# Layer 1's attention scores: split queries and keys over 128 rows instead of plain products over 64

## The chip, the cores and the metric

The kernel runs on one core of a Trainium2 chip as one program. The metric is device time in microseconds (us); the median of several executions is compared. One execution of each kernel was also recorded by the hardware profiler, and all rows below come from such a recording. Engines are named as in the profile: PE is TensorE (PEld its weight loads), DVE is VectorE, ACT is ScalarE, POOL is GpSimd, and SP issues most loads.

## The reference, cut to what matters

The network has a first block and, behind it, a second block of two layers over 256 latent tokens and 256 context tokens. The change lies in the differential attention of the second block's last layer. There are 8 heads; each has two components of 64 dimensions for queries and keys. In the last layer only the 256 latent tokens are queries, and all 512 tokens are keys.

```python
def diff_attend(q, k, v, lam):
    s = jnp.einsum('bqhcd,bkhcd->bchqk', q, k).astype(jnp.float32) * (ATT_HEAD_DIM ** -0.5)
    p = jax.nn.softmax(s, axis=-1)
    a = p[:, 0] - lam * p[:, 1]
    return jnp.einsum('bhqk,bkhe->bqhe', a.astype(v.dtype), v)
...
    att_l, att_c = diff_attention(apply_rope(qk(ql), cos, sin), apply_rope(qk(kl), cos, sin), vv(vl),
                                  qk(qc), qk(kc), vv(vc), lam, lam_init, subln_g, with_ctx_out)
```

## The kernel before

**Number forms.** The kernel keeps the accuracy of float32 in its large products by splitting both operands into a high part, rounded to the type float32r, and a low part, the rest. `mm3` (L156 to L158) then adds three products: high by high, high by low, low by high. Weights come through `slab`: a load on SP's queue into `wr`, a cast on ScalarE into `wh` (L150), a subtraction on VectorE into `wl` (L151), three buffers each. `fm` makes one such product over all 1024 input features, into a PSUM bank with the tag `lin`, of which there are two in this stage.

**The attention of a layer** is `attention`, called with `last=False` in layer 0 and `last=True` in layer 1. Layer 0 has 512 queries (four tiles of 128 in each head), layer 1 has 256 (two tiles). For each head, `proj` makes the queries (even index) and the keys (odd index) of both components, 64 rows each, in one tile of 128 rows: `fm`, a copy out of PSUM (L1030), four copies of 32 rows that swap halves (L1033), and three operations on VectorE for the rotation (L1034 to L1036). `parts` then splits this tile in layer 0. Keys: in component 0's tile, rows 0 to 63 hold the high part and rows 64 to 127 the low part, and for component 1 the other way round. Queries: one tile holds the high part twice, a second one (`lows`) holds the low part in one half and zeros in the other. Two products over 128 rows then give high by high, high by low, and low by high. In layer 1, `parts` returns the tile as it is, and `scores` multiplies it as plain float32, component 0 on rows 0 to 63, component 1 on rows 64 to 127 (L1071).

**A tile's chain.** `scores` writes two PSUM banks (tag `sc`, two buffers, so the next tile's scores wait for this tile's exponentials). `weights` takes each maximum (L1084), the exponential with its sum on ScalarE (L1086), and the combined weights on VectorE (L1088 to L1093). `values` transposes them on TensorE (L1099), copies them (L1101) and multiplies them by V (L1105). The loop over tiles (L1150) starts a tile's successor before it finishes the tile, and puts in other work for TensorE: the next projection, or `cover`, which runs steps of `ssd_out` (the output projection of the other branch, L156 to L158 with `yh` and `w_ssd_o`). `finish` normalizes a head; its transposes (L1120) are put into a later tile, for the last head behind the gate products `ga`.

**Order.** The order of instructions on each engine is set by a scheduling layer when the program is built, from all instructions and their dependences; each engine then works in that order. So an edit can move instructions far from it.

Of the kernel before, what the change touches and what calls it, by code (L numbers as in the profile page):

```python
# [9 lines left out]
F32 = mybir.dt.float32  # L10
F32R = mybir.dt.float32r
# [1006 lines left out]
def attention(C, l, H, V, neglam, gsub, ao, last, cover):  # L1018


    nc, A = C.nc, C.A
    mm = nc.tensor.matmul
    W = A["wqk"][l]
    NQ = 256 if last else 512
    nt = NQ // 128

    def proj(i, N):
        ps = C.fm([W[i]], lambda k: (H(k)[0][:, :N], H(k)[1][:, :N]), N)
        t = C.t("qk" if last else "qt", [128, N])
        nc.scalar.copy(t, ps)  # L1030
        sw = C.t("sw", [128, 256])
        for b in range(4):
            nc.scalar.copy(sw[32 * b:32 * b + 32, :], ps[32 * (b ^ 1):32 * (b ^ 1) + 32, 0:256])  # L1033
        nc.vector.tensor_tensor(t[:, 0:256], t[:, 0:256], C.cos, ALU.mult)  # L1034
        nc.vector.tensor_tensor(sw, sw, C.sin, ALU.mult)
        nc.vector.tensor_tensor(t[:, 0:256], t[:, 0:256], sw, ALU.add)  # L1036
        return t

    def parts(i, N):


        t = proj(i, N)
        if last:
            return t
        a, b = slice(0, 64), slice(64, 128)
        hi = [C.t("qk", [128, N], F32R) for _ in range(2)]
        if i % 2:
            nc.scalar.copy(hi[0][a], t[a])
            nc.vector.tensor_tensor(hi[0][b], t[a], hi[0][a], ALU.subtract)
            nc.scalar.copy(hi[1][b], t[b])  # L1050
            nc.vector.tensor_tensor(hi[1][a], t[b], hi[1][b], ALU.subtract)
            return hi
        lo = lows[i // 2 % 2]
        nc.scalar.copy(hi[0][a], t[a])
        nc.scalar.copy(hi[1][b], t[b])
        nc.scalar.copy(hi[0][b], t[a])
        nc.scalar.copy(hi[1][a], t[b])
        nc.vector.tensor_tensor(lo[0][a], t[a], hi[0][a], ALU.subtract)
        nc.vector.tensor_tensor(lo[1][b], t[b], hi[1][b], ALU.subtract)
        return hi, lo  # L1060

    def scores(q, k, tq):
        k0, nk = (0, 4) if tq < 2 else (2, 2)
        n = nk * 128
        r = []
        tok, keys = slice(tq * 128, (tq + 1) * 128), slice(k0 * 128, 512)
        for c in range(2):
            sc = C.p("sc")[:, :n]
            row = slice(c * 64, c * 64 + 64)
            if last:  # L1070
                mm(sc, q[row, tok], k[row, keys], start=True, stop=True)  # L1071
            else:
                mm(sc, q[0][c][:, tok], k[c][:, keys], start=True, stop=False)
                mm(sc, q[1][c][:, tok], k[c][:, keys], start=False, stop=True)
            r.append(sc)
        return r, k0, nk

    def weights(sc, n):
        pr = C.t("pr", [128, 2, 512])
        m = C.t("sm", [128, 2])  # L1080
        m8 = C.t("sm", [128, 2])
        den = C.t("sm", [128, 2])
        for c in range(2):
            nc.vector.tensor_reduce(m[:, c:c + 1], sc[c], AX.X, ALU.max)  # L1084
            nc.vector.tensor_scalar(m8[:, c:c + 1], m[:, c:c + 1], -0.125, None, ALU.mult)
            nc.scalar.activation(pr[:, c, :n], sc[c], AF.Exp, bias=m8[:, c:c + 1], scale=0.125, accum_out=den[:, c:c + 1])  # L1086
        r = C.t("sm", [128, 2])
        nc.vector.reciprocal(r, den)  # L1088
        rl = C.t("sm", [128, 1])
        nc.vector.tensor_tensor(rl, r[:, 1:2], neglam, ALU.mult)  # L1090
        a = C.t("at", [128, 512])
        nc.vector.tensor_scalar(a[:, :n], pr[:, 0, :n], r[:, 0:1], None, ALU.mult)
        nc.vector.scalar_tensor_tensor(a[:, :n], pr[:, 1, :n], rl, a[:, :n], ALU.mult, ALU.add)  # L1093
        return a

    def values(a, k0, nk, h, tq, ob, ss, v):
        tp = C.p("tr")
        for i in range(nk):
            nc.tensor.transpose(tp[:, i * 128:(i + 1) * 128], a[:, i * 128:(i + 1) * 128], C.ident)  # L1099
        aT = C.t("aT", [128, 512])  # L1100
        nc.scalar.copy(aT[:, :nk * 128], tp[:, :nk * 128])  # L1101
        cover()
        po = C.p("o")
        for i in range(nk):
            mm(po[:, 0:128], aT[:, i * 128:(i + 1) * 128], v[:, k0 + i, h % 2 * 128:(h % 2 + 1) * 128], start=i == 0, stop=i == nk - 1)  # L1105
        nc.scalar.copy(ob[:, tq, :], po[:, 0:128])
        jk = C.t("at", [128, 128])
        nc.scalar.activation(jk, ob[:, tq, :], AF.Square, accum_out=ss[:, tq:tq + 1])

    def finish(h, ob, ss):  # L1110
        v = C.t("sm", [128, 4])
        nc.vector.tensor_scalar(v[:, :nt], ss[:, :nt], 1.0 / 128, 1e-6, ALU.mult, ALU.add)
        r = C.rsqrt(v[:, :nt], nt)
        for tq in range(nt):
            nc.vector.tensor_scalar(ob[:, tq, :], ob[:, tq, :], r[:, tq:tq + 1], None, ALU.mult)

        def put(tag="tr"):
            tp = C.p(tag)
            for tq in range(nt):
                nc.tensor.transpose(tp[:, tq * 128:(tq + 1) * 128], ob[:, tq, :], C.ident)  # L1120
            nc.scalar.activation(ao(h), tp[:, :NQ], AF.Copy, scale=gsub)
        return put

    lows = []
    if not last:
        lows.extend([C.keep([128, NQ], F32R, name="ql") for _ in range(2)] for _ in range(2))
        for pair in lows:
            nc.gpsimd.memset(pair[0][64:128].bitcast(F32), 0.0)
            nc.gpsimd.memset(pair[1][0:64].bitcast(F32), 0.0)
    todo = [(h, tq) for h in range(8) for tq in range(nt)]  # L1130

    chunks = [(2 * h + i, (NQ, 512)[i]) for h in range(8) for i in range(2)]
    ready = {}

    def project():
        if chunks:
            i, N = chunks.pop(0)
            ready[i] = parts(i, N)

    def start(i):  # L1140
        h, tq = todo[i]
        return scores(ready[2 * h], ready[2 * h + 1], tq)

    project()
    project()
    put, vs = None, [V(0), V(1)]
    sc, k0, nk = start(0)
    if last:
        project()
    for i, (h, tq) in enumerate(todo):  # L1150
        if tq == 0:
            if h in (2, 4):
                vs.append(V(h // 2 + 1))
            ob = C.t("ob", [128, 4, 128])
            ss = C.t("sm", [128, 4])
        a = weights(sc, nk * 128)
        if tq < 2 and chunks:
            project()
        else:
            cover()  # L1160
        if tq == 0 and put:
            put()
        kk = k0, nk
        if i + 1 < len(todo):
            sc, k0, nk = start(i + 1)
        values(a, *kk, h, tq, ob, ss, vs[h // 2])
        if tq == nt - 1:
            put = finish(h, ob, ss)
    cover()
    return put  # L1170
# [36 lines left out]
def layer(C, l, pre, get_x, vec, mods, neglam, init, H, last, enter=None, sums=None):  # L1207
# [27 lines left out]
    with C.phase(f"l{l}", gT=(NQ, max(ng, 1))):  # L1235
# [90 lines left out]
        with C.phase(f"a{l}", ao=(NQ, 8), ob=(512, 2)):  # L1326
            aos = [C.t("ao", [128, NQ]) for _ in range(8)]
            C.psum(**PS["ah"])
            with C.phase(f"ah{l}", skip=24 if last else 40, V=(1024, 2), qk=(512, 8), qt=(512, 1), sw=(256, 2), pr=(1024, 2), at=(512, 3), aT=(512, 2),
                         yr=(NQ, 2), yh=(NQ, 12 if last else 11)):  # L1330
                so = ssd_out(C, l, yd, vec, T1, NQ)
                def V(j):
                    v = C.t("V", [128, 4, 256])
                    nc.gpsimd.dma_start(v, vd[:, :, j * 256:(j + 1) * 256])
                    return v

                ry = C.rstd_steps(acc, NQ, 2048, rsy)
                steps = iter(COVER[last])

                def cover():  # L1340
                    next(ry, None)
                    for _ in range(int(next(steps, 0))):
                        next(so, None)

                put = attention(C, l, H, V, neglam, gsub, lambda k: aos[k], last, cover)
                for _ in so:
                    pass
# [462 lines left out]
```

## Time and profile before

| | |
|---|---|
| three runs | 2458.41, 2455.89, 2449.28 us |
| median | 2455.89 us |
| profiled execution | 2455.91 us, of which the recorded span is 2454.1 us |
| PE busy | 2394.6 us of the span (98%), mean granted clock 0.995 |
| DVE, ACT, POOL busy | 1737.9 (71%), 1379.5 (56%), 185.6 (8%) |
| layer 1's scores (L1071) | 64 records, 2028.1 to 2174.3 us of the span |

Busy time is the union of an engine's recorded instructions. Matmuls overlap in their pipeline, so the distance between the starts of two matmuls tells what one costs, and its own duration does not. Layer 1's attention lies at about 2017 to 2190 us of the span, layer 0's at about 840 to 1072.

### The profile page before, as it was taken

Reading aid. Unit: us, or ns where it says so; the run is one execution under the profiler, and the core shown is the slowest. Engines: PE = TensorE matmul, PEld = TensorE weight load, DVE = VectorE, ACT = ScalarE, POOL = GpSimd, SP = SyncE. Lnnn points to the kernel's source line nnn. Section 1 sums busy time; section 2 is a strip of 40 time slices with the busy share of each in tenths; the row PEclk is TensorE's granted clock in tenths of the full one; section 3 lists DMA queues with packets and bytes.
Section 4 is the critical chain, followed back from the end, with each engine's and each line's share of the span. In section 5 each row is a group of like instructions: output and inputs, shape, how many; then the busy total and the mean of one; then the engine's idle time right before and its main releaser. Section 6 shows DMA issues by size and latency. Waiting matters only on the chain. (4 is left out here: it accounts for less than half of the span.)

```text
span 2454.1 us, 40285 instructions
## 1 busy us (share of the span) xinstructions
PE 2394.6 (98%) x15330; PEld 2023.8 (82%) x15330; DVE 1737.9 (71%) x3336; ACT 1379.5 (56%) x2793; POOL 185.6 (8%) x426
## 2 busy tenths in 40 slices
PE   7999999999999999999999999999999999999998
PEld 7869998877777777788888777899788887789997
DVE  6558757698888778873485334467888887887776
ACT  5445545577687677743353223245776766655553
POOL 2000000122122100000100000001211210000000
PEclk9999999999999999999999999999999999999999
DMA  7537775645545422233467553346555553346654
GB/s 272 173 129 235 254 261 167 211 133 155 155 134 170 139 82 82 78 90 95 122 234 259 169 172 135 96 154 199 181 153 161 181 163 105 103 139 206 182 187 130
DMA packets 117585, 395.53 MB, mean 161 GB/s; under 512 B 15360, under 2 KB 21232, under 8 KB 117392
## 3 DMA queue, kind: packets, MB, share of 16 engines
q1 hardware_dynamic: 96768, 328.35, 41.6%
q0 software_dynamic: 20624, 64.62, 9.5%
q8 instruction: 120, 1.97, 0.3%
q14 instruction: 73, 0.60, 0.1%
HBM read 378.34 MB, written 14.05 MB: 160 GB/s over the span
## 5 line engine op out<-in xcount | busy, mean ns | idle before, releaser
L150 ACT CAST wh<-wr 128x1024 fp32r<-128x1024 f32 (+2 forms) x509 | 530.5, 1042 | 654.5 <-PE lin L157 544.4
L151 DVE TENSOR_TENSOR wl<-wr,wh 128x1024 fp32r<-128x1024 f32 (+2 forms) x509 | 617.5, 1215 | 340.0 <-ACT wh L150 332.6
L156 PE MATMUL lin<-hh,wh 128*128 128x512 f32 (+2 forms) x1296 | 476.4, 368 | 2.3 <-ACT sw L1033 1.7
L157 PE MATMUL lin<-hl,wh 128*128 128x512 f32 (+2 forms) x1296 | 467.5, 361 | 0.3 <-DVE hl L1556 0.3
L158 PE MATMUL lin<-hh,wl 128*128 128x512 f32 (+2 forms) x1296 | 466.4, 360 | 0.1
L156 PEld LDWEIGHTS lin<-hh,wh 128*128 128x128 f32 (+1 forms) x1296 | 243.3, 188 | 48.7 <-issue 5.7
L158 PEld LDWEIGHTS lin<-hh,wl 128*128 128x128 f32 (+1 forms) x1296 | 243.0, 188 | 39.0 <-issue 1.2
L157 PEld LDWEIGHTS lin<-hl,wh 128*128 128x128 f32 (+1 forms) x1296 | 243.3, 188 | 38.3 <-issue 2.5
L889 DVE SCALAR_TENSOR_TENSOR cy<-xp,cw,cy 128x512 f32<-128x512 f32 (+1 forms) x256 | 181.4, 714 | 11.4 <-ACT cy L887 6.4
L156 PE MATMUL lin<-nh,wh 128*128 128x258 f32 (+2 forms) x576 | 185.2, 322 | 0.5 <-ACT wh L150 0.5
L158 PE MATMUL lin<-f,wl 128*128 128x256 f32 (+1 forms) x576 | 182.7, 318 | 1.8 <-DVE wl L151 1.8
L157 PE MATMUL lin<-nl,wh 128*128 128x258 f32 (+2 forms) x576 | 184.0, 319 | 0.1
L158 PE MATMUL lin<-nh,wl 128*128 128x258 f32 (+2 forms) x576 | 184.0, 320 | 0.0
L156 PE MATMUL lin<-f,wh 128*128 128x256 f32 (+1 forms) x576 | 183.7, 319 | 0.2 <-ACT f L161 0.2
L157 PE MATMUL lin<-f,wh 128*128 128x256 f32 (+1 forms) x576 | 182.8, 318 | 0.0
L156 PE MATMUL lin<-xh,wh 128*128 128x256 f32 (+1 forms) x472 | 135.2, 287 | 11.0 <-ACT wh L150 10.3
L158 PE MATMUL lin<-xh,wl 128*128 128x256 f32 (+1 forms) x472 | 132.4, 281 | 1.3 <-DVE wl L151 1.3
L157 PE MATMUL lin<-xl,wh 128*128 128x256 f32 (+1 forms) x472 | 132.3, 280 | 0.0
L156 PEld LDWEIGHTS lin<-nh,wh 128*128 128x128 f32 x576 | 109.3, 190 | 20.3 <-issue 5.0
L156 PEld LDWEIGHTS lin<-f,wh 128*128 128x128 f32 x576 | 109.2, 190 | 15.3 <-issue 3.4
L158 PEld LDWEIGHTS lin<-f,wl 128*128 128x128 f32 x576 | 109.6, 190 | 9.4 <-DVE wl L151 2.0
L158 PEld LDWEIGHTS lin<-nh,wl 128*128 128x128 f32 x576 | 109.3, 190 | 7.6 <-DVE wl L151 0.2
(444 smaller groups left out, 5274.8 us busy)
## 6 DMA issues: line engine op xcount, KB each, us to landing
wr<-in_w_mlp SPq DMA_DIRECT2D x144, 512.0 KB, 4.4
aw<-in_ada_w SPq DMA_DIRECT2D x96, 512.0 KB, 5.0
wr<-in_wxbc SPq DMA_DIRECT2D x64, 512.0 KB, 4.4
BC<-dcs POOLq DMA_DIRECT2D x96, 256.0 KB, 5.2
wr<-in_w_out SPq DMA_DIRECT2D x32, 512.0 KB, 3.7
wr<-in_wv SPq DMA_DIRECT2D x32, 512.0 KB, 4.2
EC<-der POOLq DMA_DIRECT2D x64, 256.0 KB, 5.0
wr<-in_wz SPq DMA_DIRECT2D x32, 512.0 KB, 6.3
```

Source lines behind the costliest of these rows:

```text
L150: nc.scalar.copy(hi[:, :n], raw[:, :n])
L151: nc.vector.tensor_tensor(lo[:, :n], raw[:, :n], hi[:, :n], ALU.subtract)
L156: mm(out, sh, mh, start=first, stop=False)
L157: mm(out, sh, ml, start=False, stop=False)
L158: mm(out, sl, mh, start=False, stop=last)
L889: nc.vector.scalar_tensor_tensor(cy, xp[:, :, k:k + 256], w(k), cy, ALU.mult, ALU.add)
```

## The change

Layer 1 takes the same path as layer 0. Every projection goes through the tile `qt` (one buffer) and is split into high and low parts; the eight buffers `qk` then hold two tiles for each projection instead of one. Four tiles `lows` for the queries' low parts are made, with their unused halves set to zero on GpSimd. Each component's scores are two products over 128 rows, 512 columns each, in float32r.

```diff
@@ -1026,7 +1026,7 @@
 
     def proj(i, N):
         ps = C.fm([W[i]], lambda k: (H(k)[0][:, :N], H(k)[1][:, :N]), N)
-        t = C.t("qk" if last else "qt", [128, N])
+        t = C.t("qt", [128, N])
         nc.scalar.copy(t, ps)
         sw = C.t("sw", [128, 256])
         for b in range(4):
@@ -1040,8 +1040,6 @@
 
 
         t = proj(i, N)
-        if last:
-            return t
         a, b = slice(0, 64), slice(64, 128)
         hi = [C.t("qk", [128, N], F32R) for _ in range(2)]
         if i % 2:
@@ -1066,12 +1064,8 @@
         tok, keys = slice(tq * 128, (tq + 1) * 128), slice(k0 * 128, 512)
         for c in range(2):
             sc = C.p("sc")[:, :n]
-            row = slice(c * 64, c * 64 + 64)
-            if last:
-                mm(sc, q[row, tok], k[row, keys], start=True, stop=True)
-            else:
-                mm(sc, q[0][c][:, tok], k[c][:, keys], start=True, stop=False)
-                mm(sc, q[1][c][:, tok], k[c][:, keys], start=False, stop=True)
+            mm(sc, q[0][c][:, tok], k[c][:, keys], start=True, stop=False)
+            mm(sc, q[1][c][:, tok], k[c][:, keys], start=False, stop=True)
             r.append(sc)
         return r, k0, nk
 
@@ -1121,12 +1115,10 @@
             nc.scalar.activation(ao(h), tp[:, :NQ], AF.Copy, scale=gsub)
         return put
 
-    lows = []
-    if not last:
-        lows.extend([C.keep([128, NQ], F32R, name="ql") for _ in range(2)] for _ in range(2))
-        for pair in lows:
-            nc.gpsimd.memset(pair[0][64:128].bitcast(F32), 0.0)
-            nc.gpsimd.memset(pair[1][0:64].bitcast(F32), 0.0)
+    lows = [[C.keep([128, NQ], F32R, name="ql") for _ in range(2)] for _ in range(2)]
+    for pair in lows:
+        nc.gpsimd.memset(pair[0][64:128].bitcast(F32), 0.0)
+        nc.gpsimd.memset(pair[1][0:64].bitcast(F32), 0.0)
     todo = [(h, tq) for h in range(8) for tq in range(nt)]
 
     chunks = [(2 * h + i, (NQ, 512)[i]) for h in range(8) for i in range(2)]
```

In layer 1 each even projection so has four casts of 64 x 256 on ScalarE and two subtractions of 64 x 256 on VectorE behind the rotation, each odd one two casts and two subtractions of 64 x 512. Lines behind the edit have smaller numbers after the change: L1093 and L1099 are the transposes and the value products there, L1052 to L1055 and L1046, L1048 the casts.

The scheduling layer gives TensorE, VectorE and ScalarE another order from this stage's start to its end; SP's order stays, and GpSimd's gains the four memsets alone. Two places follow. On ScalarE, where the first head's queries (`qk_21294`, after: `qt_21302`) and keys are prepared, before:

```order
L1030 COPY qk_21294<-lin_21263 128x256
L1033 COPY sw_21296<-lin_21263 32x256 x4
L1183 ACTIVATE yh_21494<-yr_21492,vec_2324 128x256
L1183 ACTIVATE yh_21500<-yr_21498,vec_2324 128x256
L150 CAST wh_21517<-wr_21516 128x1024
L1030 COPY qk_21335<-lin_21304 128x512
L1033 COPY sw_21337<-lin_21304 32x256 x4
```

The same place after the change, down to the casts of the keys:

```order
L1030 COPY qt_21302<-lin_21271 128x256
L1033 COPY sw_21304<-lin_21271 32x256 x4
L1175 ACTIVATE yh_21534<-yr_21532,vec_2324 128x256
L1175 ACTIVATE yh_21540<-yr_21538,vec_2324 128x256
L1052 CAST qk_21312<-qt_21302 64x256
L1053 CAST qk_21313<-qt_21302 64x256
L1054 CAST qk_21312<-qt_21302 64x256
L1055 CAST qk_21313<-qt_21302 64x256
L150 CAST wh_21557<-wr_21556 128x1024
L1030 COPY qt_21351<-lin_21320 128x512
L1033 COPY sw_21353<-lin_21320 32x256 x4
```

The four casts of the queries now stand ahead of the copies that empty the keys' PSUM bank. The second place is the end of the stage on TensorE: the last tile's transposes (`tr_23280`) and value products (`o_23341`), with products of `ssd_out` between them. Before:

```order
L156 MATMUL lin_23402<-yh_22997,wh_23397 128x256
L1099 MATMUL tr_23280<-c_ident,at_23250 128x128 x4
L157 MATMUL lin_23402<-yh_22998,wh_23397 128x256
L158 MATMUL lin_23402<-yh_22997,wl_23398 128x256
L156 MATMUL lin_23402<-yh_23048,wh_23397 128x256
L157 MATMUL lin_23402<-yh_23049,wh_23397 128x256
L158 MATMUL lin_23402<-yh_23048,wl_23398 128x256
L156 MATMUL lin_23402<-yh_23141,wh_23397 128x256
L157 MATMUL lin_23402<-yh_23142,wh_23397 128x256
L158 MATMUL lin_23402<-yh_23141,wl_23398 128x256
L1105 MATMUL o_23341<-V_22395,aT_23285 128x128 x4
```

After the change, from the last tile's scores (`sc_23327` and `sc_23330`) over the tile before it (`tr_23333`, `o_23380`) to its own transposes and value products (`tr_23432`, `o_23493`):

```order
L1067 MATMUL sc_23327<-qk_23075,qk_22927 128x512
L1068 MATMUL sc_23327<-qk_23075,ql_21265 128x512
L157 MATMUL lin_23568<-yh_23349,wh_23549 128x256
L158 MATMUL lin_23568<-yh_23348,wl_23550 128x256
L1067 MATMUL sc_23330<-qk_23076,qk_22928 128x512
L1068 MATMUL sc_23330<-qk_23076,ql_21266 128x512
L1093 MATMUL tr_23333<-c_ident,at_23273 128x128 x4
L1099 MATMUL o_23380<-V_22499,aT_23338 128x128 x4
L1093 MATMUL tr_23432<-c_ident,at_23402 128x128 x4
L1099 MATMUL o_23493<-V_22499,aT_23437 128x128 x4
```

All products of `ssd_out` now stand ahead of the last scores' second half; behind it the two tiles' transposes and value products follow each other, and then the gate products `ga`.

## Rows read from the trace of the kernel before

**Rows 1.** The page's first part, TensorE's share of it.

```profile
PE 2394.6 (98%) x15330; PEld 2023.8 (82%) x15330; DVE 1737.9 (71%) x3336; ACT 1379.5 (56%) x2793; POOL 185.6 (8%) x426
```

**Rows 2.** Windows: length, busy PE, PEld, DVE, ACT, POOL, PEclk, DMA, GB/s.

```profile
2017.00:2190.00 173.00, 164.11 (x1025) 132.64 (x1024) 135.66 (x373) 115.54 (x272) 3.04 (x5) 0.99 0.39 121
840.00:1072.00 232.00, 222.55 (x1117) 174.05 (x1116) 187.24 (x520) 171.81 (x420) 1.50 (x2) 1.00 0.27 83
2020.00:2030.00 10.00, 7.07 (x39) 4.91 (x38) 5.67 (x10) 7.19 (x15) 0.00 (x0) 0.93 0.71 242
```

**Rows 3.** Timeline of TensorE, layer 1: start, duration, line, tiles, shape, [idle before].

```profile
2062.99 0.28 PE L157 MATMUL lin<-hl,wh 128*128 128x256 f32 x1
2063.11 0.28 PE L158 MATMUL lin<-hh,wl 128*128 128x256 f32 x1
2063.31 1.13 PE L1071 MATMUL sc<-qk,qk 64*128 64x512 f32 x4
2064.37 0.39 PE L156 MATMUL lin<-yh,wh 128*128 128x256 f32 x1
2064.59 0.28 PE L157 MATMUL lin<-yh,wh 128*128 128x256 f32 x1
...
2173.73 1.12 PE L1071 MATMUL sc<-qk,qk 64*128 64x512 f32 x2
2174.78 0.39 PE L157 MATMUL lin<-yh,wh 128*128 128x256 f32 x1
```

**Rows 4.** Line L1071: its window (PE, PEld busy), and TensorE's idle time before it.

```profile
2017.00:2190.00 173.00, 23.07 (x64) 7.21 (x64) 0.99 0.39 121
...
  ACT pr L1086: 3.5, 8
```

**Rows 5.** Timeline of TensorE, layer 0's first scores.

```profile
844.36 0.50 PE L1073 MATMUL sc<-qk,qk 128*128 128x512 f32 x1 [0.61 <-DVE qk L1049]
844.70 0.40 PE L1074 MATMUL sc<-qk,ql 128*128 128x512 f32 x1
844.93 0.40 PE L158 MATMUL lin<-yh,wl 128*128 128x512 f32 x1
```

**Rows 6.** Tile qt, layer 0: ns min/median/max, first and last start.

```profile
L1048 ACT CAST qk<-qt x8: 602/617/623, 842.6 to 1028.7; 64x512 fp32r<-64x512 f32 x8
L1049 DVE TENSOR_TENSOR qk<-qt,qk x8: 684/685/686, 843.6 to 1029.8; 64x512 fp32r<-64x512 f32 x8
```

**Rows 7.** Lines by form, 2190 to 2200 us: busy us, mean ns | idle before.

```profile
L161 ACT CAST ah<-ao 128x256 fp32r<-128x256 f32 x8 | 2.9, 404 | 0.0
L162 DVE TENSOR_TENSOR al<-ao,ah 128x256 fp32r<-128x256 f32 x8 | 3.4, 426 | 0.0
```

**Rows 8.** Waits, 2017 to 2190 us: us in total, times, longest.

```profile
ACT pr L1086 <- DVE sm L1085: 28.9, 12, 3.9
DVE sm L1088 <- ACT pr L1086: 13.2, 13, 2.0
```

**Rows 9.** Timeline of TensorE at the stage's start.

```profile
2025.52 0.50 PE L156 MATMUL lin<-hh,wh 128*128 128x512 f32 x1 [1.51 <-ACT sw L1033]
...
2030.67 0.63 PE L156 MATMUL lin<-hh,wh 128*128 128x512 f32 x1
2031.10 0.63 PE L157 MATMUL lin<-hl,wh 128*128 128x512 f32 x1
```

**Rows 10.** Timeline of VectorE and TensorE, the last tile's chain.

```profile
2179.78 1.28 DVE L1084 TENSOR_REDUCE sm<-sc 128x1 f32<-128x512 f32 x2
...
2184.81 0.60 PE L1099 MATMUL tr<-c_ident,at 128*128 128x128 f32 x4
2185.16 0.37 PE L157 MATMUL lin<-yh,wh 128*128 128x256 f32 x1
...
2186.36 1.16 PE L1105 MATMUL o<-V,aT 128*128 128x128 f32 x8
2187.28 0.36 PE L156 MATMUL lin<-yh,wh 128*128 128x256 f32 x1
```

## The prediction

> **What bounds the kernel now.** The page's first part comes first: TensorE is busy for 98% of the span [rows 1], so a change pays only where it shortens TensorE's own work or a wait of TensorE. The windows view then cuts out the stage that the change touches, layer 1's attention, from 2017 to 2190 us of the span [rows 2]. Of these 173 us TensorE is busy for 164.1, VectorE for 135.7, ScalarE for 115.5. So TensorE is idle for 8.9 us here, and 2.9 of them lie in the first ten, where the first heads' queries and keys are prepared (7.07 of 10 busy). The other 6.0 are spread over sixteen tiles. Layer 0's attention already works in the split form, and the same view shows it from 840 to 1072 us: TensorE 222.6 of 232, idle 4.1%, with VectorE at 81% and ScalarE at 74%. It is the nearest thing to a trace of the changed kernel.
>
> **What the scores cost TensorE now.** A tile (128 queries of a head) has two plain products, one on rows 0 to 63 and one on rows 64 to 127, each recorded as two matmuls. Four records together hold TensorE for 1.06 us, from 2063.31 to the next start at 2064.37, and the one product that stands alone at 2173.73 holds it for 1.05 [rows 3]. So the two halves run at the same time, and a pair costs what one costs. Around a pair the stream stumbles: starts are 0.12 us apart in the stream, but 0.20 going in and 0.22 coming out, some 0.19 too much. All of the scores keep TensorE busy for 23.1 us [rows 4]. That is more than 16 x 1.06 = 17, because in several tiles the second half waits for the exponentials to free its bank: 3.5 us of waits in 8 places [rows 4], more inside the pairs. There are 17 groups (the last tile's halves stand apart). Each record ends about 0.07 after the next may start, so the scores take 23.1 - 17 x 0.07 + 17 x 0.19 = 25.1 us of TensorE's time.
>
> **What they cost after.** Layer 0 shows the new form: after the first product, which takes 0.34 behind a wait, the starts are 0.23 apart for 512 columns [rows 5]. A tile has four (two components, high and low queries): 64 x 0.23 = 14.7 us, and 16 x 0.11 for the first of each tile makes 16.5. The saving is at most 25.1 - 16.5 = 8.6 us. At least it is what the pairs cost without waits: 16 x (1.06 + 0.19) = 20.0, less 16.5, that is 3.5, if every wait inside a pair comes back as a wait between the new products. I take the middle, 6.
>
> The Trainium skill speaks against the change here: "TensorEngine Tiling (Array Packing)", Theoretical Speedup, gives up to 2x where the contracted dimension is 64 or less, and products over 128 rows give that up. The trace agrees that the two halves overlap (1.06 for both, 1.05 for one). The same page, Key Properties, says that a switch of the tiling mode drains TensorE, which agrees with the 0.20 and 0.22 beside 0.12. By the first rule together with "FP8 and Floating Point Precision", TensorE Precision Notes (true FP32 is four passes), streaming alone would be 4 x 512 columns before and after, a saving of nothing but the switches.
>
> **What is added on ScalarE and VectorE.** For each head the queries need four casts on 64 x 256 and two subtractions, the keys two casts on 64 x 512 and two subtractions. Layer 0 has the key's sizes: 0.617 us a cast, 0.686 a subtraction [rows 6]. No row has 64 x 256; between 128 x 256 (0.404 and 0.426 [rows 7]) and 64 x 512 (0.617 and 0.686) I take the lower, since the columns agree, and keep the upper for the range. ScalarE: 8 x (4 x 0.404 + 2 x 0.617) = 22.8 us. VectorE: 8 x (2 x 0.426 + 2 x 0.686) = 17.8 us (21.9 at the upper end). The stage would then have VectorE at (135.7 + 17.8)/173 = 89% and ScalarE at 80%: above layer 0's 81% and 74%, and below full. Both have gaps to put this in: 13.2 us in which VectorE waits for the exponentials and 28.9 in which ScalarE waits for the maxima [rows 8]. The cover is there on the average but not at every tile, since both engines work in order. If TensorE's idle share in the tiles goes from 6.0/163 = 3.7% towards twice layer 0's 4.1%, it costs between 0.7 and 7.4 us. I take 2, near layer 0's share, as its work is the same in kind.
>
> The queue of SP issues the same loads in the same order. GpSimd's four memsets stand ahead of the loads of V on its queue; the first value products come only after a whole tile's softmax, so they cost nothing. The copy into qt has one buffer now; layer 0 works with the same one, and its list of waits names no copy waiting for a subtraction. Nothing.
>
> **The start of the stage.** On ScalarE the four casts of the first queries are put ahead of the copies that free the bank of the first keys (the order listing of ScalarE). In the trace TensorE waits 1.51 us for just these copies, until 2025.52 [rows 9]. Four casts of 0.404 move that to 2027.1: 1.6 us more. After the wait the matmuls start 0.43 apart instead of 0.23 [rows 9], in a stretch with a mean granted clock of 0.93 [rows 2]: the lower level, 1.2 GHz, after idle time. That exists already. The first scores then wait for casts and subtractions of the keys, but ten products of the next projection now stand ahead of them, where it was four. I take 1.6, with 0.5 and 4 as the ends.
>
> **The end of the stage.** This is the piece that the diff alone doesn't show. Before, 51 projection products stand between the last two tiles (from the value products of the one to the transposes of the other), and more before and behind. After, they are used up earlier: behind the last scores come only two transposes and two value products, with nothing between (the order listing of TensorE). From the last tile's maxima at 2179.78 to the end of its value products, 0.92 us after 2186.36, the chain takes 7.5 us in the trace [rows 10]. TensorE has left to do there: 0.46 of scores, two transposes of 0.35 and two value products of 0.92, 3.0 us. So 4.5 us are idle. The finish of the last head then has 48 products (5.5 us) as cover where it had 63 (7.2 us): 0.5 more. Sum 5, between 3 (without the filler that VectorE ran inside that chain) and 8 (if the clock falls as at the start).
>
> **Sum.** -6 + 2 + 1.6 + 5 = +2.6 us. The profiled execution took 2455.91 us (span 2454.1, 1.8 around it) and the median of the three runs is 2455.89, so no correction: **2458 us**. The three runs lie 9 us apart, and about 0.5% (12.3 us) is what a measurement of this kernel can tell from no change.
>
> **The rivals.**
> *A, the work is hidden and TensorE keeps its gain.* No more idle time in the tiles, 8.6 saved, 1.6 at the start, 3 at the end: -4, 2452 us. For it: the gaps of [rows 8]. Against it: the last tile's bare chain. Chance 0.25.
> *B, VectorE becomes the bound.* Its idle time was 173 - 135.7 = 37.3 us. In my forecast the stage lasts 175.6 us and VectorE needs 153.5, so its idle time must shrink to 22.1. If none of it can be filled, because each wait for an exponential stays in the order, the stage grows by 17.8: 2474 us, slower by 0.7%. It decides for slower by 0.5% from 32 us of idle time on. For it: VectorE at 89% in order. Against it: layer 0 runs at 81% and loses 4.1% on TensorE. Chance 0.17, of which 0.1 is beyond 0.5%.
> *C, the products gain nothing but the switches.* If the four products of a tile take the pair's 1.06 us, because of waits between them, TensorE saves 16 x (0.19 - 0.11) = 1.3 us: 2455.9 - 1.3 + 8.6 = 2463 us. The streaming rule of the Trainium skill above would give this. For it: the waits for banks. Against it: the 0.23 of [rows 5]. Chance 0.15.
> My forecast has 0.43, with a range of its own from 2454 to 2463.
>
> **How the numbers follow.** The range reaches 3 us below A and 2 above half of B (2455.9 + 8.9 = 2465), for the spread of the runs: 2449 to 2467. Slower by over 0.5% (above 2468.2) is B's worse part, 0.10. Faster by over 0.5% (below 2443.6) needs all of the 8.6 and much of the idle 8.9 as well: 0.04. The rest, 0.86, is within.
>
> **What would show it.** In the trace after: the scores' products 0.23 apart, about 16 us in sum; VectorE near 153 us in the stage; TensorE's wait for the copies at the start about 3 us; a hole of 4 to 5 us in TensorE between the last scores and the gate products. I am wrong if VectorE's queue holds up the weights' low parts (waits of the third product of a group), if the hole is not there, or if a wait for a tile of the stage before shows up at the first copies, since the new tiles move the others in memory.

## The result, and the profile after

Six executions of the changed kernel had a median of 2478.63 us (2477.02 to 2481.99), and six of the kernel before 2453.2. The ratio is 1.0106, with a 95% interval from 1.009 to 1.0121: slower by 1.1%, about 25 us. The forecast was 2458, within 2449 to 2467.

The first part of the page of the changed kernel answers to [rows 1]:

```profile
PE 2394.7 (97%) x15330; PEld 2031.7 (82%) x15330; DVE 1751.6 (71%) x3368; ACT 1403.1 (57%) x2841; POOL 186.8 (8%) x430
```

TensorE's busy time is the same as before (2394.7 and 2394.6 us), while the span grew from 2454.1 to 2476.3 us. So the 22 us are idle time of TensorE; that its busy time did not fall, although the score products got shorter, is taken up below. The windows view of the changed kernel (columns as in [rows 2]) shows where, for the stage and for ten microseconds at its end:

```profile
2013.00:2212.00 199.00, 165.78 (x1025) 141.32 (x1024) 153.95 (x413) 139.34 (x323) 4.20 (x9) 0.95 0.35 109
2199.00:2209.00 10.00, 3.58 (x19) 2.71 (x19) 6.31 (x18) 3.29 (x9) 0.00 (x0) 0.64 0.22 77
```

TensorE is idle for 33.2 us of the stage, where it was 8.9. VectorE is busy for 154 us, as worked out (153.5), but in 199 us that is 77%, and ScalarE is at 70%. No engine is full. VectorE is idle for 45.0 us, where it was 37.3, and ScalarE for 59.7, where it was 57.5: the added work did not go into their idle time.

The lines by form of the changed kernel from 2013 to 2215 us show that the sizes were right: casts of 0.406 and 0.621 us, subtractions of 0.423 and 0.687 (forecast: 0.404, 0.617, 0.426, 0.686).

```profile
L1049 DVE TENSOR_TENSOR qk<-qt,qk 64x512 fp32r<-64x512 f32 x8 | 5.5, 687 | 0.3
...
L1046 ACT CAST qk<-qt 64x512 fp32r<-64x512 f32 x8 | 5.0, 621 | 2.2 <-DVE qt L1036 2.1
...
L1057 DVE TENSOR_TENSOR ql<-qt,qk 64x256 fp32r<-64x256 f32 x8 | 3.4, 423 | 0.3
...
L1054 ACT CAST qk<-qt 64x256 fp32r<-64x256 f32 x8 | 3.2, 406 | 0.2
```

What TensorE waits for now is seen in the list of waits of the changed kernel, 2013 to 2215 us (total, times, longest):

```profile
ACT wh L150 <- PE lin L157: 15.3, 11, 2.6
DVE sm L1106 <- ACT at L1102: 15.0, 6, 4.8
...
PE lin L156 <- ACT sw L1033: 9.9, 8, 2.0
ACT pr L1080 <- DVE sm L1079: 8.7, 5, 3.5
...
PE tr L1093 <- DVE at L1087: 7.6, 4, 4.4
...
DVE sm L1082 <- ACT pr L1080: 6.5, 11, 1.1
PE lin L156 <- DVE T L1195: 5.7, 6, 2.4
PE sc L1067 <- ACT pr L1080: 5.5, 7, 1.5
```

Rows of the kernel before to set beside them, 2017 to 2190 us:

```profile
ACT wh L150 <- PE lin L157: 7.1, 5, 2.1
...
DVE sm L1112 <- ACT at L1108: 2.3, 2, 1.9
...
PE sc L1071 <- ACT pr L1086: 1.0, 2, 0.7
```

The rows of `ACT pr` and of `DVE sm L1082` answer to [rows 8]: ScalarE's waits for the maxima shrank from 28.9 us to 8.7, VectorE's for the exponentials from 13.2 to 6.5. Other waits took their place, ScalarE's for products that free a weight buffer (7.1 to 15.3) and VectorE's for the sums of the finish (2.3 to 15.0), so that the idle time as a whole grew. TensorE now waits 9.9 + 5.7 us for copies and additions that empty the `lin` banks, where it was the 1.51 at the start [rows 9], and 5.5 in seven places for the exponentials, where it was 1.0 in two (of the 3.5 in [rows 4], 2.5 belong to the weight loads). One of these waits, on the timelines of ScalarE and of TensorE in the changed kernel:

```profile
2029.67 1.04 ACT L150 CAST wh<-wr 128x1024 fp32r<-128x1024 f32 x1
2030.61 0.40 ACT L1052 CAST qk<-qt 64x256 fp32r<-64x256 f32 x1
...
2031.88 0.40 ACT L1055 CAST qk<-qt 64x256 fp32r<-64x256 f32 x1
2032.31 0.51 ACT L1175 ACTIVATE yh<-yr,vec 128x256 fp32r<-128x256 f32 x1
2032.73 0.57 ACT L1030 COPY qt<-lin 128x512 f32<-128x512 f32 x1
2033.32 1.49 ACT L1033 COPY sw<-lin 32x256 f32<-32x256 f32 x4
```

```profile
2032.58 0.28 PE L158 MATMUL lin<-yh,wl 128*128 128x256 f32 x1
2034.86 0.39 PE L156 MATMUL lin<-hh,wh 128*128 128x256 f32 x1 [2.00 <-ACT sw L1033]
```

ScalarE has no gap here. The four casts of the next queries (1.7 us) stand ahead of the copies that free the bank, and TensorE waits 2.00 us for the last of them. The two waits at the start of the stage, which answer to [rows 9]:

```profile
2021.85 0.50 PE L156 MATMUL lin<-hh,wh 128*128 128x512 f32 x1 [2.00 <-ACT sw L1033]
...
2025.67 0.50 PE L1067 MATMUL sc<-qk,qk 128*128 128x512 f32 x1 [0.53 <-DVE qk L1047]
```

The end of the stage, on TensorE's timeline of the changed kernel, answers to [rows 10]:

```profile
2195.69 0.39 PE L1067 MATMUL sc<-qk,qk 128*128 128x512 f32 x1
2195.92 0.39 PE L1068 MATMUL sc<-qk,ql 128*128 128x512 f32 x1
2196.15 0.28 PE L157 MATMUL lin<-yh,wh 128*128 128x256 f32 x1
...
2199.64 0.63 PE L1093 MATMUL tr<-c_ident,at 128*128 128x128 f32 x4 [2.30 <-DVE at L1087]
2200.94 1.27 PE L1099 MATMUL o<-V,aT 128*128 128x128 f32 x8 [0.68 <-ACT aT L1095]
2206.64 1.09 PE L1093 MATMUL tr<-c_ident,at 128*128 128x128 f32 x4 [4.43 <-DVE at L1087]
2208.41 1.86 PE L1099 MATMUL o<-V,aT 128*128 128x128 f32 x7 [0.68 <-ACT aT L1095]
```

The score products start 0.23 us apart, as forecast. The hole is there: 2.30 + 0.68 + 4.43 + 0.68 = 8.1 us, with a mean granted clock of 0.64 in the window around it.

### The profile page after: what moved, and what is told of

It is laid out like the page before. It is cut to its first block, busy times and chain, and to the rows that moved or that the text cites. A ratio compares the mean times of both kernels' runs of the same rounds, so it can differ in the third digit from the quotient of the medians.

```text
span 2476.3 us, 40391 instructions
## 1 busy us (share of the span) xinstructions
PE 2394.7 (97%) x15330; PEld 2031.7 (82%) x15330; DVE 1751.6 (71%) x3368; ACT 1403.1 (57%) x2841; POOL 186.8 (8%) x430
## 5 line engine op out<-in xcount | busy, mean ns | idle before, releaser
L156 PEld LDWEIGHTS lin<-nh,wh 128*128 128x128 f32 x576 | 109.3, 190 | 19.9 <-ACT wh L150 4.3
L156 PEld LDWEIGHTS lin<-f,wh 128*128 128x128 f32 x576 | 109.3, 190 | 15.3 <-ACT wh L150 3.4
```

The source lines that it names most:

```text
L156: mm(out, sh, mh, start=first, stop=False)
```

## The experiments

**How they are compared.** Profiled executions differ by up to 15 us outside this stage, in code that the edits leave as it is. So beside each ratio stands the length of the stage in the trace: from the start of the first copy of layer 1's query projection to the start of the first product that reads `ah`. It is 177.4 us before (2017.56 to 2194.92) and 203.2 after (2013.53 to 2216.73). All ratios are to the kernel before, with their 95% intervals; the experiments ran on five chips, each beside runs of the kernel before on its own. A stage is read from one execution, and how much it varies between executions of one kernel was not measured. It and the ratio can disagree: x7's stage is 4.5 us shorter than before, while its ratio shows no gain.

| run | median us | ratio | interval | stage us |
|---|---|---|---|---|
| *order free, as the scheduling layer sets it* | | | | |
| the change | 2478.63 | 1.0106 | 1.0090 to 1.0121 | 203.2 |
| e1 split, plain products | 2480.21 | 1.0102 | 1.0076 to 1.0127 | 203.2 |
| e2 products alone | 2463.74 | 1.0032 | 1.0016 to 1.0048 | 187.3 |
| e3 more buffers | 2482.27 | 1.0133 | 1.0101 to 1.0164 | 207.4 |
| e4 low parts on GpSimd | 2492.20 | 1.0162 | 1.0140 to 1.0184 | 217.5 |
| e8 three lin banks | 2480.61 | 1.0101 | 1.0084 to 1.0119 | 204.5 |
| *TensorE in the written order* | | | | |
| b kernel before | 2475.04 | 1.0081 | 1.0066 to 1.0096 | 199.4 |
| e6 products alone | 2477.05 | 1.0089 | 1.0076 to 1.0103 | 199.9 |
| e7 split, plain products | 2492.40 | 1.0155 | 1.0139 to 1.0171 | 215.7 |
| e5 the change | 2497.94 | 1.0178 | 1.0165 to 1.0191 | 219.0 |
| *three engines in the order of before* | | | | |
| x1 products alone | 2451.57 | 0.9987 | 0.9974 to 0.9999 | 176.2 |
| x2 the change | 2474.98 | 1.0080 | 1.0062 to 1.0098 | 197.3 |
| x3 split, plain products | 2476.71 | 1.0087 | 1.0070 to 1.0105 | 199.8 |
| x4 casts alone | 2471.28 | 1.0067 | 1.0053 to 1.0080 | 193.0 |
| x5 subtractions alone | 2468.85 | 1.0057 | 1.0040 to 1.0074 | 187.5 |
| x6 half the split, three products | 2461.89 | 1.0033 | 1.0020 to 1.0046 | 184.6 |
| x7 one product, no split | 2457.33 | 1.0009 | 0.9997 to 1.0020 | 172.9 |
| *order of before, transposes later* | | | | |
| y1 one product | 2452.06 | 1.0000 | 0.9987 to 1.0013 | 178.6 |
| y2 kernel before | 2454.28 | 0.9998 | 0.9988 to 1.0009 | 179.3 |

### The two halves of the change, and two remedies (e1 to e4)

```diff
# e1: the change, with
+ mm(sc, q[0][c].bitcast(F32)[row, tok], k[c].bitcast(F32)[row, keys], start=True, stop=True)
# e2: the kernel before, with
- t = C.t("qk" if last else "qt", [128, N])
+ t = C.t("qk" if last else "qt", [128, N], F32R if last else F32)
- mm(sc, q[row, tok], k[row, keys], start=True, stop=True)
+ mm(sc, q[:, tok], k[:, keys], start=True, stop=False)
+ mm(sc, q[:, tok], k[:, keys], start=False, stop=True)
# e3: the change, with
- qk=(512, 8), qt=(512, 1)
+ qk=(512, 16 if last else 8), qt=(512, 2 if last else 1)
# e4: the change, with
+ low = nc.gpsimd if last else nc.vector
+ low.tensor_tensor(...)      (the four subtractions)
```

> The casts and subtractions stay in layer 1, the products are plain float32 ones over 64 rows again, on the high parts (the low parts are computed and left out of the scores). Theory L (the added work on ScalarE and VectorE holds up the copies that empty the lin banks and the exponentials): TensorE's waits stay and its saving goes, so slower than the change by about 6 us, 2480 to 2486. Theory P (the loss comes from the four products themselves, which wait for banks and tiles): near the kernel before, 2453 to 2460.

> Layer 1's scores are made by products over 128 rows, but queries and keys aren't split: the rotation writes float32r tiles, and each component's product runs twice over the same rows (the scores so mix both components). Theory L: TensorE's saving alone, 4 to 8 us faster than the kernel before, 2445 to 2449. Theory P: most of the loss is here, 2470 or more.

> The change, with two qt tiles in place of one and 16 qk tiles in place of 8, in layer 1. Theory Q (one qt tile, and qk tiles for two heads in place of four, make projections wait for the split of the one before): most of the 25 us come back, 2455 to 2463. Theory L: no more than 3 us come back, 2475 to 2480.

> The change, with layer 1's subtractions for the low parts on GpSimd, which is busy for 8% of the span. Theory L with VectorE as the engine that matters: 12 to 20 us come back, 2459 to 2467. Theory L with ScalarE as the engine that matters: 0 to 5 us come back, 2474 to 2479. If GpSimd slows VectorE down, or is so slow that the scores wait for it: slower, above 2485.

The split without its products costs as much as the whole change (2480.21). That speaks for theory L. But the saving of TensorE that the change should have over it (about 6 us) doesn't show, and the products without the split cost 8 us by the ratio and 10 in the stage, which neither theory allows: nothing is added there on any other engine. On TensorE's timeline of e2 the hole at the end is there too:

```profile
2194.17 0.63 PE L1100 MATMUL tr<-c_ident,at 128*128 128x128 f32 x4 [4.44 <-DVE at L1094]
2195.47 1.86 PE L1106 MATMUL o<-V,aT 128*128 128x128 f32 x7 [0.68 <-ACT aT L1102]
```

So an edit of the products alone seems to make the scheduling layer choose an order that loses time; x1 below bears that out. More buffers bring nothing back. On GpSimd a subtraction on 64 x 512 took 1.28 and 1.47 us on the average of its two lines, where VectorE takes 0.69, and the stage grew by 14 us more. The Trainium skill, "GPSIMD Engine Reference", 4.1 Engine selection, gives about twice VectorE's time for operations with two inputs; these rows agree. Both remedies also changed the order, so their numbers don't tell the load from the order.

### The order by itself (b, e5 to e7)

To tell the two apart, the order was held. A function at the end of `attention` adds edges between an engine's instructions that set only the order in which they are issued; here TensorE's follow as the program writes them.

```diff
+ for prev, ins in zip(seq, seq[1:]):
+     C.tc.add_manual_dep(ins, prev.name, mybir.DependencyInfo(mybir.DependencyClass.NoSync, ...))
```

> The kernel before, with TensorE's instructions of layer 1's attention held in the order in which the program writes them. Control for the three others: the order listing of before is nearly this order already, so both theories expect 2448 to 2460, no measurable change.

> The change, with TensorE's instructions of layer 1's attention held in the order in which the program writes them, so that the steps of the output projection stay behind the tiles that they are written for. Theory O (the order that the scheduling layer chose after the edit is the loss: filler is drawn forward, in front of waits for PSUM banks, and is missing at the end): most of the 25 us come back, 2450 to 2462. Theory L (the added work on ScalarE and VectorE is the loss): 2472 to 2480, the hole at the end filled and the rest as it was.

> The products over 128 rows on unsplit queries and keys (as in the second experiment, so the scores mix both components), with TensorE held in the written order. Theory O: the 10 us that the products alone cost come back and the saving of TensorE shows, 2444 to 2450. If the products themselves wait for something: 2458 or more.

> The split with plain products over 64 rows on the high parts (as in the first experiment; the low parts are left out of the scores), with TensorE held in the written order. Theory O: 2453 to 2462. Theory L: 2472 to 2482. The difference to the change in the written order is what the products are worth, 4 to 8 us.

The control was wrong: the kernel before, with the same instructions, became 20 us slower by the ratio. The written order differs from the one that it had in few places, above all these: the first scores stand 28 products earlier, the transposes of eight tiles 1 to 11, and those of the last two 40 and 55. On its timeline of TensorE the first of these places costs 7.47 us, where it was 1.42:

```profile
2029.58 1.23 PE L1071 MATMUL sc<-qk,qk 64*128 64x512 f32 x2 [7.47 <-DVE qk L1036]
```

So theory O can't be judged by this order, but the four kernels can be compared in it: the products alone cost 0.5 us in the stage (199.9 to 199.4), the split 16.3, both 19.6.

### The change in the order of the kernel before (x1 to x3), and a third bank (e8)

Now TensorE, VectorE and ScalarE were held in exactly the order of the kernel before. A score product of it became two, one behind the other; the added casts and subtractions were left for the scheduling layer to place between the others. e8 is the change in its free order with one edit:

```diff
- C.psum(**PS["ah"])
+ C.psum(**(dict(sc=2, lin=3, tr=2, o=1) if last else PS["ah"]))
```

> The products over 128 rows on unsplit queries and keys (the scores mix both components), with TensorE, VectorE and ScalarE of layer 1's attention held in exactly the order of the kernel before. Theory O (the order chosen after an edit is the loss): the 10 us of the second experiment vanish and a saving shows, 2445 to 2452. If shorter products only lengthen the waits behind them: 2453 to 2457. If the products themselves cost time: 2460 or more.

> The whole change, with TensorE, VectorE and ScalarE of layer 1's attention held in the order of the kernel before; only the added casts and subtractions are placed by the scheduling layer between them. Theory O: most of the 25 us vanish, 2453 to 2462, and the end has its filler again. Theory L (the added work, in an in-order engine, holds up what stands behind it): 2468 to 2480; the hole at the end vanishes (5 to 8 us) and the waits for the lin banks and the exponentials stay.

> The split with plain products over 64 rows on the high parts (the low parts are left out of the scores), with the three engines in the order of the kernel before, the added work between. Theory O: 2453 to 2462. Theory L: 2470 to 2480, at most 6 us more than the change in the same order.

> The change, with three PSUM banks for lin in layer 1's attention in place of two (the bank of the small sums is given up; they share the transposes' banks). Theory B (the two lin banks, emptied late by ScalarE, are where the added work turns into waits of TensorE, 13 of the 24 us of new idle time): 10 to 15 us come back, 2463 to 2469. If the delay only moves to the next dependence (exponentials, keys): under 4 us, 2475 to 2480.

In one and the same order the products bring the stage from 177.4 to 176.2 us, the split to 199.8, both to 197.3. x1 is theory O's, at the edge of its range (the loss of e2 is gone, the saving is small), and x2 and x3 are theory L's. So the split costs some 22 us, the products give back 1.2 (x1) to 2.5 (x2 against x3), and together they are 19.9 of the change's 25.8; about 6 (203.2 to 197.3) are the order's, and the hole at the end is gone in x2. The windows view over the whole stage (columns as in [rows 2]) of the kernel before, x1, x2 and the change:

```profile
2017.56:2194.92 177.36, 168.47 (x1064) 137.09 (x1064) 140.41 (x390) 118.40 (x280) 2.48 (x4) 0.99 0.40 121
2016.24:2192.41 176.17, 161.79 (x1065) 140.98 (x1064) 140.35 (x390) 118.41 (x280) 2.49 (x4) 0.99 0.39 122
2012.30:2209.55 197.25, 167.14 (x1065) 141.38 (x1064) 157.33 (x421) 140.24 (x328) 3.76 (x7) 0.98 0.36 109
2013.53:2216.73 203.20, 169.98 (x1064) 145.61 (x1063) 158.40 (x430) 141.54 (x330) 3.76 (x7) 0.95 0.34 106
```

In x2 VectorE is idle for 39.9 us and ScalarE for 57.0, where it was 37.0 and 59.0 before: the 17 and 22 us that they have more to do found almost no idle time to go into. TensorE is idle for 15.7 us more in x2 than in x1. By their lists of waits 6.0 of them lie in front of the scores (for the exponentials), 5.0 at `lin` banks that an addition or a copy on the helpers has to empty, 2.0 at the first keys, 1.9 at the transposes and 1.0 at the value products.

e8 brought nothing back, but it doesn't tell whether the banks are a cause: its order is another, and in its trace (2015 to 2218 us) TensorE waits for the copies no less than with two banks:

```profile
PE lin L156 <- ACT sw L1033: 11.2, 7, 5.8
```

That projections wait for the one tile `qt` or for the tiles `qk` (theory Q) is hardly seen in x2: its list of waits has one such wait of ScalarE, 1.5 us (`ACT qt L1030 <- DVE qk L1049`).

x2 shows how the delay arises where the order is good. The timelines of VectorE, ScalarE and TensorE in x2 (the last three rows are one of ScalarE, one of TensorE's scores, and the product behind it):

```profile
2037.48 0.69 DVE L1047 TENSOR_TENSOR qk<-qt,qk 64x512 fp32r<-64x512 f32 x1 [0.36 <-ACT qk L1046]
2038.20 0.69 DVE L1049 TENSOR_TENSOR qk<-qt,qk 64x512 fp32r<-64x512 f32 x1
...
2040.17 1.28 DVE L1081 TENSOR_REDUCE sm<-sc 128x1 f32<-128x512 f32 x2
```

```profile
2041.54 0.69 ACT L1083 ACTIVATE pr<-sc,sm 128x512 f32<-128x512 f32 x1 [2.73 <-DVE sm L1082]
```

```profile
2042.37 0.50 PE L1069 MATMUL sc<-qk,qk 128*128 128x512 f32 x1 [2.13 <-ACT pr L1083]
2042.71 0.40 PE L1070 MATMUL sc<-qk,ql 128*128 128x512 f32 x1
```

VectorE waits for a cast (0.36) and makes two subtractions (1.38) ahead of small operations and the maxima. Meanwhile ScalarE stands still for 2.73 us, in order, in front of the exponential, and TensorE for 2.13 in front of the next scores, whose bank the exponential has to free. Neither helper is full (VectorE 78%, ScalarE 73% of 2012 to 2190 us by the windows view), and yet the added instructions delay the chain that TensorE waits for. They stand where the scheduling layer put them; other places in the same order were not tried.

### Which half of the split, and what shorter scores bring (x4 to x7)

```diff
# x4: x3 without the four subtractions
# x5: the plain products of before on tiles qt (eight buffers), and for each projection two of
+ nc.vector.tensor_tensor(hi[0][b], t[a], t[a], ALU.subtract)
# x6: one cast and one subtraction for a projection, three products
+ nc.scalar.copy(hi[0], t)
+ nc.vector.tensor_tensor(hi[1], t, hi[0], ALU.subtract)
+ mm(r[c], q[j // 2][row, tok], k[j % 2][row, keys], start=j == 0, stop=j == 2)
# x7: the plain product of before on tiles that the rotation writes as F32R
```

> The casts alone, with plain products over 64 rows on the high parts (no low parts at all), the three engines in the order of the kernel before. Theory S (ScalarE, in order, is where the added work holds up the exponentials and the copies that empty banks): 13 to 20 us above the kernel before, 2467 to 2476. Theory V (VectorE, the busier engine, is it): 0 to 6 above, 2454 to 2460. Both alike: about 10 above, 2463 to 2466.

> The subtractions alone: as many of the same sizes as in the change, of a tile from itself, their results unused, with the plain products of the kernel before and the three engines in its order. Theory S: 0 to 6 us above the kernel before, 2454 to 2460. Theory V: 13 to 20 above, 2467 to 2476.

> Another split for layer 1: one cast and one subtraction over 128 rows for a projection, and for each component three float32r products over 64 rows (high by high, high by low, low by high), the two components on the two halves of the rows in turn; the three engines in the order of the kernel before. The added casts are 8.2 us in place of 22.8, the subtractions 8.9 in place of 17.8. If the cost follows the added time on ScalarE and VectorE: about 40 per cent of 20 us, less 3 to 5 for the products, 2456 to 2461. If it is the longer chain from projection to scores that costs: 2466 or more.

> No split: the rotation writes float32r tiles, and each component has a single float32r product over 64 rows (the low parts are left out of the scores), the three engines in the order of the kernel before. A pair takes about 0.3 us of TensorE in place of 1.06, some 12 us less in sixteen tiles. If TensorE keeps it: 2440 to 2445. If the scores are cover for the softmax of the tile before and most comes back as waits of the transposes: 2448 to 2453, no better than the experiment with two products.

Neither engine is the one: x4 is in theory S's range, x5 in theory V's. The casts (22.8 us of ScalarE's time by the prediction's sum) lengthen the stage by 15.7 us, the subtractions (17.8 of VectorE's) by 10.1, both together by 22.5, a little less than the sum of 25.8. Which of the two costs more the times don't tell: the intervals of x4 and x5 overlap. Nothing waits for x5's results, so its cost is that of the place in the queue alone. Less than half of the work costs a third: x6 adds 8.2 + 8.9 = 17.1 us and lengthens the stage by 7.2, with three products in place of x3's plain ones, so that this is not the load alone. The cost goes roughly with the added time, about half of it: 22.5 of 40.6, and 7.2 of 17.1.

x7 is the other half of the answer. Its products take the least time of all on TensorE (it is busy for 156.0 us of the stage, 12.5 less than before), and the kernel is not faster (1.0009). The list of waits shows where most of it went; that the profiled execution still has a stage shorter by 4.5 us is not explained. The transposes' row in the kernel before (2017 to 2190 us):

```profile
PE tr L1099 <- DVE at L1093: 3.1, 6, 0.6
```

the same row in x1 (2016 to 2192):

```profile
PE tr L1101 <- DVE at L1095: 8.2, 13, 0.9
```

and in x7 (2020 to 2192):

```profile
PE tr L1099 <- DVE at L1093: 12.3, 14, 1.2
```

The scores of the next tile stand between a tile's own scores and its transposes. They are part of the cover under which VectorE makes the weights, and what they save is waited for behind them: 5.1 us more in x1, 9.2 in x7.

### Filler in front of the transposes (y1, y2)

In the order table of before, each tile's four transposes were moved behind the next six filler products (fifteen tiles; behind the last there is none).

> One rounded product over 64 rows and no split (the low parts are left out of the scores), in the order of the kernel before, but each tile's four transposes stand six products of 128 x 256 or 128 x 512 later on TensorE, so that filler lies between the scores and the transposes. If the waits for the weights took the gain (0.5 to 1.2 us in each of fifteen tiles, 13 us in all): 8 to 12 us of them go, less what the value products then wait for the copy of the transposes, 2445 to 2451. If the tile's chain through VectorE and ScalarE sets the pace: 2454 to 2458, the wait only moves to the value products.

> The kernel before with the same shift of the transposes. Its waits there are 0.55 us in eight tiles, some 4 us in all: 2449 to 2453 if they go, 2454 to 2458 if they move to the value products.

Neither gained. The list of waits of y1 (2015 to 2190 us) shows the wait one step further on, at the value products, and at the bank of the filler that follows:

```profile
PE lin L156 <- ACT sw L1033: 7.6, 7, 4.0
PE o L1105 <- ACT aT L1101: 6.7, 9, 1.4
```

4.0 of the 7.6 us are one wait at the start of the stage. At the transposes 1.4 are left of the 12.3 us of x7; the other 3.6, and 5.5 more at the value products (6.7, where x7 has 1.2), take most of their place. y1's median lies between its two expectations, y2's in the second. The waits fit the second, a tile's way through VectorE and ScalarE being as long as TensorE's own work; it was not measured by itself. No version that computes the scores beats the kernel before by more than the intervals allow.

## Why the prediction was wrong

- **"-6" for the products.** The mechanism was right (0.23 us apart, no switch of the row halves) and the gross size as well (TensorE is busy for 6.7 us less in x1's stage), but it was put down as a gain. In the order of before it left 1.2 us in the stage, or 0.13% of the time (x1): 5.1 us came back as waits of the transposes. The prediction named the waits in front of the scores, and not those behind them for which the scores are cover. In the change nothing of it is left: TensorE is busy for 165.8 us where it was 164.1. Part of the stage ran at the lower clock (mean granted clock 0.95, before 0.99), and a product behind a wait holds TensorE longer (0.34 to the next start at 2042.37 in x2, where the stream has 0.23); how much each took was not separated.
- **"+2" for idle time in the tiles.** This is the step that failed. TensorE is idle for 33.2 us in the stage; without the start (2.00 + 0.53) and the hole (8.1) 22.6 remain, where it was 6.0. So the term was +17. The step counted on the helpers' idle time as room, but that time did not shrink: VectorE's went from 37.3 to 45.0 us. Layer 0's idle share [rows 2] was taken for the price of its split, but it only tells what is idle with the split, and layer 0 has four tiles to a head where layer 1 has two, so that half as many projections fall on a tile (a reason that no run tested). ScalarE at 80% and VectorE at 89% "below full" was no protection: the work goes into in-order queues in front of the maxima, the exponentials and the copies. Measured at one order (x3 to before, x2 to x1), it costs 21 to 22 us of the stage.
- **"+1.6" at the start.** The two waits were 2.00 + 0.53 us, against 1.51 + 1.42: nothing was lost there.
- **"+5" at the end.** The hole was seen in the order listing and is there, at 8.1 us, the upper end, with the clock at 0.64. The half microsecond for the finish behind it did not show as a wait. The hole is the order's doing, as x2 has none. With it the terms add up, as measured from 2013 to 2212 us: +1.7 - 0.4 + 16.6 + 8.1 = 26.0 us for products, start, tiles and end, which is the growth of the window from 173 to 199 us.
- **Rival B** came closest in time (2474), and for a reason that holds only in part. It named VectorE as the bound; VectorE is at 77%, and the casts on ScalarE, which the prediction thought covered, cost 15.7 us by themselves. What it had right is its condition: VectorE's idle time was not filled, and in x2 the stage grew by 19.9 us where VectorE had 16.9 more to do.
- **Rival A** had the gaps of [rows 8] as cover. Those two kinds of waits shrank (28.9 to 8.7 us, 13.2 to 6.5), but others grew, and in x2 they are about as long as before (33.8 and 12.8). **Rival C** gave the products 1.3 us, and x1 left 1.2, but not for its reason: the four products take less than the pair, and the rest is lost behind them, not between them.
- **Two readings** of the prediction are off, without weight: the 3.5 us of [rows 4] are mostly the weight loads' (TensorE's matmuls waited 1.0), and 0.20 + 0.22 - 2 x 0.12 is 0.18, not 0.19.

What stays open is how much of the 6 us between the change and x2 is the hole, the clock and the other places; and why e3, e4 and e8 moved the time as they did, since each also changed the order.

## What to carry to other kernels

Where the engine that seems to be the bound idles for only 5% of a stage, its helpers may still be as much of a bound through the order of their queues: about half of each microsecond added on ScalarE and VectorE came through here, with both no more than 80% busy, and in the order of before their idle time hardly shrank. Before counting a shorter product as a gain, look at what stands behind it and what that waits for; a product can be the cover of a softmax. And where a scheduling layer sets the order, hold the order of before when testing one half of a change: the same instructions in a slightly different order differed by 20 us here, where the whole change cost 25.

## What was not expected

- The time outside the stage varied from 2269 to 2285 us between the profiled executions, in code that the edits leave as it is, so that a single time tells less than the stage's length (x5's and x6's profiled executions, the longest there, were 5 and 10 us above their medians).
- Casts and subtractions cost more together than either, but not their sum (22.5 against 15.7 + 10.1 us in the stage, 0.87% against 0.67% + 0.57% in time). That they delay the same chain would explain it; no run shows it.
